# Gated linear attention loop: the score matrix of a token block computed in 64-token pieces, two of them side by side in the array

## The chip, the cores and the metric

The kernel runs on one core of one Trainium2 chip. The metric is device time in microseconds of one execution; lower is better. The time before is 1255.59 us, the median of three runs (1254.0 to 1257.15).

## The reference, cut to what matters

The program is one step of a two-layer backbone on 256 context tokens and 1024 latent tokens of width 1024. Layer 0 mixes tokens by gated linear attention (4 heads, key width 128, value width 256, both directions over the tokens), layer 1 by grouped-query softmax attention. The change is in layer 0. For a chunk of tokens the reference computes, with `b` the running sum of the log decays:

```python
qe = qi * jnp.exp(b)
ke = ki * jnp.exp(-b)
a = jnp.where(mask, jnp.einsum("bhtk,bhsk->bhts", qe, ke), 0.0)
o = jnp.einsum("bhts,bhsv->bhtv", a, vi) + jnp.einsum("bhtk,bhkv->bhtv", qe, S)
```

`a` is the score of each query token t against each key token s, kept where s is not after t (in the other direction: not before t). The kernel works on blocks of 128 tokens, so of the 128 x 128 scores of a block and direction one half is masked away, and one 64 x 64 quarter of it lies wholly in the masked half.

## The kernel before

The stages follow each other: modulation vectors and the first normalisation (to about 76 us), the loop `gla` of layer 0 (to about 518 us), the output projection of layer 0 with the first keys and queries of layer 1 (`gla_out`), the attention of layer 1 (`attention`), its output projection. The change touches the loop alone; the order of the instructions differs up to the first tiles of `gla_out` and is the same, instruction for instruction, from there on.

`gla` runs over head slots h = 0 to 4 and, in each, over the 10 token blocks of 128 (two of the context, eight latent). One step does, for head h: `intra` (the scores `a` and the transposed decayed keys of the block), `outer` and `local` (state update and first direction's output), and ahead of time `decay`, `decayed` and `value_gate` of later blocks; for head h - 1 it does `combine` (the other direction's scan, with its output matmul at L826) and `gated`. In h = 4 only `combine` of head 3 and the gates are left. Between these go projections for the next head (`qk_piece`), and a `filler`: matrix-vector products for the modulation (`gemv`, L391: eight f32 matmuls with weights of 32 columns, each in one of four column tiles of the array, by `tile_position=(0, 32 * j)`), weight splits, and the first output tiles. In the loop 40 blocks (4 heads x 10) call `intra`.

`intra` takes one PSUM bank of tag `kt` (one buffer): its first half receives the two transposed `ke` (L742), its second half, `ap`, the scores of both directions (L745). `ks` copies the first half out (L748), `copy_predicated` takes the unmasked scores (L753), GpSimd adds the directions (L754).

The names in the profile: `en` is `ke`, `kt` the bank, `wada` the gemv's weights, `Sc` the other direction's state, `oghl` and `hT_hi` parts of the output projection's input. L214 is the helper that issues the three f16 products of every split projection.

An f32 matmul shows in the trace as two passes, each with its own weight load; an f16 one as a single pass. PE is TensorE's matmuls, PEld its weight loads.

The order of the instructions on each engine is set by a scheduler that works on priorities (`TC = {"schedule_with_timeline_sim": True}`): code inside `with self.later("A"):` has its priority moved by `LATER["A"]`. So a changed number there, or a changed operation, moves instructions all through the loop.

Of the kernel before, what the change touches and what calls it, by code (L numbers as in the profile page):

```python
# [17 lines left out]
P = 128  # L18
# [5 lines left out]
NTP = TP // P  # L24
# [23 lines left out]
SECOND = 1  # L48

LATER = {  # L50
    "loc": -30,
    "kt": 30,
    "A": -15,
    "intra": -5,
    "ks": -90,
    "combine": -15,
    "cs": -20,
    "vg": -10,
    "u": 75,
    "gated": 50,  # L60
    "decay": -25,
    "outer": 10,
    "Uc": -100,
    "a9.qr": 30,
    "a.s1": 30,
    "gate": -5,
# [4 lines left out]
    "x.q": -15,  # L71
    "a0.qr": 40,
    "x.prep": -90,
    "oa": 30,
    "jobs": -20,
    "a.q": -210,
    "x.mod": 60,
# [6 lines left out]
    "a9.s1": -160,  # L84
    "a0.s1": 400,
    "pieces8": 95,
    "filler": -30,
    "a0.s0": 75,
    "at": -100,
    "a0.rest": 30,  # L90
# [23 lines left out]
    "eprep": 400,  # L114
    "z.out": -5,
    "x.kset": -30,
}

ADA = tuple((0, b) for b in (8, 9, 10, 11)) + tuple((1, b) for b in (4, 5, 6, 7, 0, 1, 2, 3, 8, 9, 10, 11))
# [8 lines left out]
class K:  # L128
# [603 lines left out]
    def intra(self, i, st):  # L732
        nc = self.nc
        ke, qe = st["ke"], st["qe"]
        kt, ap = (
            t.rearrange("p (d k) -> p d k", d=2)
            for b in (self.bank("kt"),)
            for t in (b[:, 0 : 2 * P], b[:, 2 * P :])
        )
        with self.later("kt"):  # L740
            for d in range(2):
                nc.tensor.transpose(kt[:, d, :], ke[:, d, :], self.ident)  # L742
        with self.later("A"):
            for d in range(2):
                nc.tensor.matmul(ap[:, d, :], ke[:, d, :], qe[:, d, :], start=True, stop=True)  # L745
        ks = self.t(self.ew, [P, 2, P], F32, "ks")
        with self.later("ks"):
            nc.vector.tensor_copy(ks, kt)  # L748
        am = self.am[self.ia % len(self.am)]
        self.ia += 1  # L750
        at = self.t(self.tl, [P, P], F32, "at", bufs=2)
        with self.later("at"):
            nc.vector.copy_predicated(am, self.mask, ap)  # L753
            nc.gpsimd.tensor_tensor(at, am[:, 0, :], am[:, 1, :], ALU.add)  # L754
        st["at"], st["ks"] = at, ks
# [108 lines left out]
    def gla(self, wq, w, filler):  # L864
# [6 lines left out]
        def ahead_decay(slot):  # L871
            h, n = divmod(slot, NT)
            if h < GH:
                g[slot] = self.decay(h, orders[h][n])
# [7 lines left out]
        def ahead_gate(slot):  # L882
# [7 lines left out]
                    self.inv_g[h - 1] = self.mulcol(self.inv_h, ws[h][2][1], self.gcp, f"inv_g{h % 2}")  # L890
            x[slot] = self.value_gate(h, orders[h][n], ws[h])

        for n in range(3):
            ahead_decay(n)
        ahead_decayed(0)
# [606 lines left out]
def emit(ctx, tc, I, O, dbg=None, stop=None):  # L1502
    k = K(ctx, tc, I, O, dbg)
    nc = tc.nc
# [27 lines left out]
    with ExitStack() as c:  # L1532
# [9 lines left out]
        with ExitStack() as c1:  # L1542
# [10 lines left out]
            def group(gi):  # L1553
                xs = []
                for j in range(GROUPS[gi][1]):
                    x = k.t(k.p1, [P, D], F32, "x", bufs=4)
                    load(x, xrow(I, GROUPS[gi][0] + j))
                    xs.append(x)
                return xs

            xs = group(0)
# [3 lines left out]
            for t in (*k.wtile(1)[0:2], *k.wtile(2)[0:2], k.hT_hi, k.hT_hi, k.hT_lo, k.hT_lo):  # L1565
                a = 4096 * (len(to) % 2) if len(to) > 3 else 0
                t = t.rearrange("p k n -> p (k n)")[:, a : a + 4096].bitcast(F32)
                n = len(to)
# [64 lines left out]
        wo, gm, prep, held, xs = [], [], [], [], []  # L1633


        def prompt(slot):
            h = [late[1][:, 512 * j : 512 * j + 512] for j in range(4)]
            if slot == 0:
                for kk in range(KT):
                    k.modulate(k.transpose(zs, kk, ("o", "U")[kk % 2]), kk, GROUPS[2][0], h=h[kk % 4])  # L1640
            elif slot < 3:
                k.qk_piece(0, slot - 1, 2, wq)
            else:
                k.rank_sum(*k.rank(2, h[0]))

        def filler(slot):
            if slot < 4:
                prompt(slot)
            if slot == 0:
                k.jobs.append(late_qk)  # L1650
            if slot == 2:
                k.fold_qk(1, wq)
            if slot in (9, 34):
                gm.append(k.mod_load(*((0, 2, 1) if slot == 9 else (1, 0, 3))))
            if slot in (10, 35):
                k.jobs.append(((k.gate_rows if slot == 10 else k.mod_rows_out), *gm.pop()))
            if slot % 2 == 0:
                if held:
                    k.gemv(*held.pop())
            elif queue:  # L1660
                held.append(k.ada_load(*queue.pop(0), k.t(k.ada, [P, KT, 256], F32, "wada")))
            if cols and slot in AHEAD:
                with tc.issue_after(first):
                    name, j, ap = cols.pop(0)
                    k.jobs.append((k.split_ahead, name, j, k.stage(ap)))
            if slot in WO:
                b = WO.index(slot)
                if b == 0:
                    k.w0 = k.wtile(0)
                if b < 2:  # L1670
                    t = [t[:, :, 256 * b : 256 * b + 256] for t in k.w0[0:2]]
                elif b == 2:
                    t = [t[:, :, 0:256] for t in k.nw[0:2]]
                else:
                    t = k.t(k.ada, [P, KT, 256], F32, "wada").rearrange("p k n -> p (k n)").bitcast(F16)
                    t = t.rearrange("p (j k n) -> p j k n", j=2, k=KT)
                    t = [t[:, 0], t[:, 1]]
                wo.append([*t, None])
                st = k.stage(I["gla_w_out"][b])
                k.jobs.append((k.placed, f"wo{b}", k.fill_out, wo[-1], st))  # L1680
            if slot == 40:
                k.gt = k.gate_load(0)
                k.iw = k.t(k.const, [P, 4], F32, "iw")
                for b, t in enumerate(wo):
                    nc.vector.tensor_copy(k.iw[:, b : b + 1], t[2])
                wo[:] = [(*k.w0[0:2], 512)] + [(hi, lo, 256) for hi, lo, _ in wo[2:]]
                t, k.gb = k.wtile(2)[0:2]
                t = t.rearrange("p k n -> p (k n)").bitcast(F32)
                for n in range(2):
                    xs.append(t[:, D * n : D * n + D])  # L1690
                    load(xs[n], xrow(I, NTP + n))
                k.rows_load(1)
            if slot in PREP:
                n = PREP.index(slot)
                a = k.t(k.wst, [P, KT, 256], F32, "wst").rearrange("p k n -> p (k n)")[:, 0:D]
                b = [k.t(k.qkp, [P, 512], F32, f"{j}{n % 2}").bitcast(F16) for j in "qk"]
                to = k.out_load(NTP + n, a, b)
                k.jobs.append((lambda *a: prep.append(k.placed("eprep", k.out_prep, *a)), *to))
            if slot in EARLY:
                n = EARLY.index(slot)  # L1700
                hT, lT, inv = prep[n]
                with k.later("eres"):
                    k.residual(
                        NTP + n, lambda j: (hT[:, j, :], lT[:, j, :]), wo, inv, xs[n], [k.bank("A"), k.bank("kt")]
                    )
                t = k.t(k.spl, [P, 2, KT // 2, 256], F16, "split").rearrange("p j k n -> p j (k n)")
                k.jobs.append((k.placed, "emod", k.early_mod, NTP + n, xs[n], (t[:, 0], t[:, 1])))

        k.gla(wq, wv, filler)
    if "og" in k.dbg:  # L1710
        load(k.dbg["og"], k.og_d)
# [3 lines left out]
    with ExitStack() as ca:  # L1715
# [15 lines left out]
        wo = []  # L1731
# [16 lines left out]
def xrow(I, i):  # L1748
    if i < NTP:
        return I["x_prompt"][0, i * P : i * P + P, :]  # L1750
    return I["x_sample"][0, (i - NTP) * P : (i - NTP) * P + P, :]
# [97 lines left out]
```

## Time and profile before

| | before |
|---|---|
| median of 3 runs | 1255.59 us (1254.0 to 1257.15) |
| profiled execution | 1256.39 us, its span 1254.6 us |
| mean granted TensorE clock | 0.993 |
| PE busy in the span | 1193.2 us (95%) |
| DVE, ACT, POOL busy | 942.8, 689.5, 326.6 us |
| the loop between 100 and 490 us | PE busy 388.46 of 390 us |
| L745 (scores), passes of PE | 160, mean 276 ns |

PE time in the profile is the union of modelled matmul spans, which overlap: a pass of 276 ns can follow the one before it after 110 ns. What a pass costs is therefore read from the distance between starts, not from its duration.

### The profile page before, as it was taken

To read this page: it belongs to the slowest core of one execution; us is meant where nothing else is said; L and a number is where in the kernel's file an instruction comes from. 1 tells how busy PE (TensorE), PEld (TensorE's weight loads), DVE (VectorE), ACT (ScalarE), POOL (GpSimd) and SP (SyncE) were. 2 spreads that over 40 slices of the span, in tenths; PEclk is the share of its full clock that TensorE was granted. 3 is DMA by queue.
4 is the path that set the end of the run, shared out by engine and by line. 5 is a ranking of instruction groups with operands and counts; after the bars stand their busy time and mean duration, and the time that the engine had idled before them with its cause. 6 is when DMAs were issued, how large, how long until landed. Compare 5 with 4: busy or idle time off the path is not lost. (4 is left out here: it accounts for less than half of the span.)

```text
span 1254.6 us, 22383 instructions
## 1 busy us (share of the span) xinstructions
PE 1193.2 (95%) x7990; PEld 781.4 (62%) x7990; DVE 942.8 (75%) x2188; ACT 689.5 (55%) x1698; POOL 326.6 (26%) x566
## 2 busy tenths in 40 slices
PE   4899999999999999898999899999999999989998
PEld 3467765655556557665776666767766657665444
DVE  4787879879788799769875687877766687785653
ACT  2664666647656567623333577666676676663110
POOL 0132123223321243311213434332232342310000
PEclk9999999999999999899999999999999999999999
DMA  9511565456555545589974887767868466978432
GB/s 377 194 65 73 202 210 191 160 176 207 164 180 179 159 124 164 142 237 248 260 191 130 182 157 132 140 132 151 185 135 151 110 123 132 195 139 208 163 135 84
DMA packets 317664, 209.74 MB, mean 167 GB/s; under 512 B 257094, under 2 KB 294254, under 8 KB 309232
## 3 DMA queue, kind: packets, MB, share of 16 engines
q1 hardware_dynamic: 310400, 190.78, 59.1%
q10 hardware_dynamic: 4688, 10.57, 2.4%
q0 software_dynamic: 2464, 6.95, 1.9%
q8 instruction: 63, 1.03, 0.3%
q14 instruction: 49, 0.40, 0.1%
HBM read 107.57 MB, written 39.35 MB: 117 GB/s over the span
## 5 line engine op out<-in xcount | busy, mean ns | idle before, releaser
L214 PEld LDWEIGHTS <-hT_hi 128*128 128x128 f16 x1920 | 187.8, 98 | 120.6 <-DMA hT_hi<-oghl 3.8
L214 PE MATMUL mm<-whi,hT_hi 128*128 128x512 f16 (+1 forms) x576 | 200.2, 348 | 0.5 <-ACT gx L679 0.4
L214 PE MATMUL mm<-whi,hT_lo 128*128 128x512 f16 (+1 forms) x576 | 200.3, 348 | 0.0
L214 PE MATMUL mm<-wlo,hT_hi 128*128 128x512 f16 (+1 forms) x560 | 194.2, 347 | 0.9 <-DVE wlo L276 0.9
L214 PEld LDWEIGHTS <-whi 128*128 128x128 f16 x1232 | 120.2, 98 | 63.8 <-issue 4.4
L1285 PE MATMUL S<-kT,wst 128*128 128x512 f16 (+1 forms) x624 | 140.2, 338 | 7.1 <-ACT p L1293 6.1
L214 PE MATMUL mm<-hT_hi,whi 128*128 128x256 f16 (+1 forms) x480 | 141.0, 294 | 3.7 <-ACT gx L1328 2.4
L1318 DVE SCALAR_TENSOR_TENSOR phl<-p,srec,phl 128x1280 f16<-128x1280 f32 (+1 forms) x80 | 107.0, 1337 | 49.5 <-ACT phl L1317 33.3
L214 PE MATMUL mm<-hT_lo,whi 128*128 128x256 f16 (+1 forms) x480 | 141.0, 294 | 0.0
L214 PE MATMUL mm<-hT_hi,wlo 128*128 128x256 f16 (+1 forms) x480 | 141.0, 294 | 0.0
L214 PEld LDWEIGHTS <-hT_lo 128*128 128x128 f16 x960 | 94.2, 98 | 62.5 <-issue 1.3
L214 PE MATMUL mm<-PT,vh 128*128 128x256 f16 x672 | 117.9, 279 | 9.3 <-DMA PT<-phl 6.3
L1288 DVE TENSOR_REDUCE smx<-S 128x1 f32<-128x1280 f32 (+1 forms) x80 | 101.3, 1271 | 27.0 <-PE S L1285 26.9
L1293 ACT ACTIVATE p<-S,snb,sexp 128x1280 f32<-128x1280 f32 (+1 forms) x80 | 99.1, 1238 | 12.6 <-DVE phl L1318 7.2
L1285 PEld LDWEIGHTS <-wst 128*128 128x128 f16 x624 | 60.9, 98 | 57.3 <-issue 7.1
L214 PE MATMUL mm<-PT,vl 128*128 128x256 f16 x336 | 93.9, 279 | 0.0
L1315 POOL TENSOR_SCALAR phl<-p,srec 128x1280 f16<-128x1280 f32 (+1 forms) x40 | 52.8, 1319 | 107.0 <-DVE srec L1309 62.7
L214 PEld LDWEIGHTS <-vh 128*128 128x128 f16 x672 | 66.7, 100 | 21.1 <-issue 6.0
L214 PEld LDWEIGHTS <-wlo 128*128 128x128 f16 x616 | 60.2, 98 | 29.8
L1124 POOL TENSOR_TENSOR rope<-hx,ropet 128x64 f32<-128x64 f32 x160 | 53.3, 363 | 84.0 <-ACT hx L1249 61.6
L237 DVE TENSOR_REDUCE wmx<-wst 128x1 f32<-128x512 f32 x104 | 65.1, 675 | 3.0 <-DMA wst<-in_att_w 2.0
L205 POOL TENSOR_TENSOR hrs<-hrsa,mhalf 128x2 f32<-128x2 f32 x50 | 39.5, 792 | 81.2 <-DVE hrsa L203 80.7
(383 smaller groups left out, 2682.7 us busy)
## 6 DMA issues: line engine op xcount, KB each, us to landing
wada<-in_w_ada SPq DMA_DIRECT2D x16, 1024.0 KB, 5.4
wst<-in_att_w SPq DMA_DIRECT2D x14, 1024.0 KB, 5.4
wst<-in_gla_w_in SPq DMA_DIRECT2D x12, 1024.0 KB, 5.3
og_d<-gx SPq DMA_DIRECT2D x40, 128.0 KB, 1.9
og_d<-og POOLq DMA_DIRECT2D x40, 128.0 KB, 3.0
wst<-og_d SPq DMA_DIRECT2D x5, 1024.0 KB, 6.1
xr<-x_d SPq DMA_DIRECT2D x9, 512.0 KB, 3.8
out<-xr ACTq DMA_DIRECT2D x17, 256.0 KB, 2.0
```

Of the source, the lines that this page charges most:

```text
L205: nc.gpsimd.tensor_tensor(r, a, self.mhalf[:, 0:w], ALU.pow)
L214: self.pe = self.nc.tensor.matmul(out, a, b, start=k == 0 and j == 0, stop=k == n - 1 and j == 2).ins
L237: nc.vector.tensor_reduce(mx[:, j : j + 1], st[:, 2 * j : 2 * j + 2, :], AX.XY, ALU.max, apply_absolute_value=True)
L1124: nc.gpsimd.tensor_tensor(tv[:, h, :, w, :], xv[:, h, :, 1 - w, :], sn[:, :, w, :], ALU.mult)
L1285: nc.tensor.matmul(S[:, a : a + n], x, y, start=m == 0, stop=m == 2)
L1288: last = nc.vector.tensor_reduce(mx, S, AX.X, ALU.max).ins
L1293: nc.scalar.activation(p, S, AF.Exp, scale=self.sexp, bias=nb, accum_out=den)
L1315: nc.gpsimd.tensor_scalar(hi, p, r, 2.0 ** 14, ALU.mult, ALU.mult)
L1318: nc.vector.scalar_tensor_tensor(lo, p, r2, hi, ALU.mult, ALU.subtract)
```

## The change

The full product of 128 keys by 128 queries becomes, for each direction, a matmul of all 128 keys by the 64 queries that need both halves of the keys, and one of 64 keys by the other 64 queries, which sits in one half of the array's columns (`tile_position=(0, 64 * d)`); the halves of the two directions are different ones. The quarter that the mask removes is set to zero once ahead of the loop. For that the bank `kt` is taken once and kept (`self.kt`). Eleven numbers of `LATER` change or are new.

```diff
 LATER = {
-    "loc": -30,
+    "loc": -5,
-    "A": -15,
-    "intra": -5,
+    "A": -30,
+    "intra": -150,
...
+    "decayed": 5,
+    "z": -100,
 }
...
         kt, ap = (
             t.rearrange("p (d k) -> p d k", d=2)
-            for b in (self.bank("kt"),)
+            for b in (self.kt,)
             for t in (b[:, 0 : 2 * P], b[:, 2 * P :])
         )
...
         with self.later("A"):
+            h = P // 2
             for d in range(2):
-                nc.tensor.matmul(ap[:, d, :], ke[:, d, :], qe[:, d, :], start=True, stop=True)
+                b = slice(h - h * d, P - h * d)
+                nc.tensor.matmul(ap[:, d, b], ke[:, d, :], qe[:, d, b], start=True, stop=True, skip_group_check=True)
+            for d in range(2):
+                b = slice(h * d, h * d + h)
+                nc.tensor.matmul(
+                    ap[b, d, b], ke[:, d, b], qe[:, d, b], start=True, stop=True,
+                    tile_position=(0, h * d), skip_group_check=True,
+                )
...
+        self.kt = self.bank("kt")
+        ap, h = self.kt[:, 2 * P :], P // 2
+        self.nc.vector.memset(ap[h:P, 0:h], 0.0)
+        self.nc.vector.memset(ap[0:h, P + h :], 0.0)
         for n in range(3):
             ahead_decay(n)
```

Three places show what moves in the order of PE's instructions. Line numbers of the changed kernel are two higher up to L745, and ten higher from L754 on: L744 is the transpose, L749 the matmul of 64 queries by all keys, L752 the quarter, L393 the gemv, L836 the output matmul of `combine`, L216 the projections.

A block in the middle of the loop (head 2, fifth of its ten), before: PE's transposes (`kt<-ident`) and scores (`kt<-qe,en`) among a projection into `mm`.

```order
L214 LDWEIGHTS hT_hi_73
L214 MATMUL mm_4362<-whi_711_2930,hT_hi_73 128x512
L742 MATMUL kt_4325<-ident_81,en_4205 128x128
L214 LDWEIGHTS hT_hi_73
L214 MATMUL mm_4362<-wlo_712_2931,hT_hi_73 128x512
L742 MATMUL kt_4325<-ident_81,en_4205 128x128
L745 MATMUL kt_4325<-qe_4210,en_4205 128x128 x2
L214 LDWEIGHTS hT_lo_74
L214 MATMUL mm_4362<-whi_711_2930,hT_lo_74 128x512
```

The same block in the changed kernel.

```order
L216 LDWEIGHTS hT_hi_73
L216 MATMUL mm_4254<-whi_697_2948,hT_hi_73 128x512
L744 MATMUL kt_794<-ident_81,en_4232 128x128 x2
L749 MATMUL kt_794<-qe_4237,en_4232 128x64 x2
L752 MATMUL kt_794<-qe_4237,en_4232 64x64 x2
L216 LDWEIGHTS hT_hi_73
L216 MATMUL mm_4254<-wlo_698_2949,hT_hi_73 128x512
L216 LDWEIGHTS hT_lo_74
L216 MATMUL mm_4254<-whi_697_2948,hT_lo_74 128x512
```

The two score matmuls have become four, and the quarters stand between instructions that use the whole array. After the 40 pairs of quarters an f16 weight load follows 25 times, a gemv 5 times, and an f32 or bf16 weight load 10 times.

A gemv, before, in PE's order in head 1, between a projection and the next block's decay sums (`cs`).

```order
L214 LDWEIGHTS hT_lo_74
L214 MATMUL mm_2555<-whi_328_1521,hT_lo_74 128x512
L391 MATMUL mm_2637<-wada_2497,cst_166 32x256 x8
L719 LDWEIGHTS ghi_2406
L719 MATMUL cs_2672<-cum_142,ghi_2406 128x130
L719 LDWEIGHTS glo_2407
L719 MATMUL cs_2672<-cum_142,glo_2407 128x130
```

The same gemv in the changed kernel.

```order
L393 MATMUL mm_2653<-wada_2512,cst_166 32x256 x3
L744 MATMUL kt_794<-ident_81,en_2549 128x128 x2
L696 LDWEIGHTS r_140
L696 MATMUL z_2558<-wa_28_141,r_140 128x256
L393 MATMUL mm_2653<-wada_2512,cst_166 32x256 x3
L749 MATMUL kt_794<-qe_2554,en_2549 128x64 x2
L752 MATMUL kt_794<-qe_2554,en_2549 64x64 x2
L393 MATMUL mm_2653<-wada_2512,cst_166 32x256 x2
```

The gemv's eight matmuls now stand in three pieces, with full-width matmuls and a pair of quarters between them. Over the loop the 16 gemvs stand in 17 pieces before and in 24 now.

The end of the loop (head slot 4), before: PE's output matmuls of `combine` (from `Sc` into the banks o, U, z, cs in turn), between projections for the gates.

```order
L214 LDWEIGHTS hT_lo_74
L214 MATMUL mm_6748<-whi_1555_5986,hT_lo_74 128x256
L826 MATMUL o_6680<-Sc_6676,qe_6278 128x256
L826 MATMUL U_6731<-Sc_6727,qe_6141 128x256
L826 MATMUL z_6786<-Sc_6782,qe_6010 128x256
L826 MATMUL cs_6855<-Sc_6851,qe_5893 128x256
L826 MATMUL o_6920<-Sc_6916,qe_5759 128x256
L214 LDWEIGHTS hT_hi_73
L214 MATMUL mm_6817<-whi_1555_5986,hT_hi_73 128x256
```

The same place in the changed kernel, up to the first matmul that has come between; 24 such matmuls of a gate projection (128x256) stand there.

```order
L216 LDWEIGHTS hT_lo_74
L216 MATMUL mm_6736<-whi_1521_6024,hT_lo_74 128x256
L836 MATMUL o_6723<-Sc_6719,qe_6319 128x256
L836 MATMUL U_6774<-Sc_6770,qe_6181 128x256
L216 LDWEIGHTS hT_hi_73
L216 MATMUL mm_6791<-whi_1521_6024,hT_hi_73 128x256
```

Behind the last of the 24 it goes on like this.

```order
L216 LDWEIGHTS hT_lo_74
L216 MATMUL mm_6791<-whi_1521_6024,hT_lo_74 128x256
L836 MATMUL z_6829<-Sc_6825,qe_6049 128x256
L836 MATMUL cs_6898<-Sc_6894,qe_5931 128x256
L836 MATMUL o_6963<-Sc_6959,qe_5796 128x256
L216 LDWEIGHTS hT_hi_73
L216 MATMUL mm_6860<-whi_1521_6024,hT_hi_73 128x256
```

One gate projection has moved from behind the five output matmuls to between the second and the third. The gate projections of the last blocks all end earlier than before, and on SyncE's queue the last store of a gated block (`og_d<-gx`) now stands ahead of the reloads for the output projection (`og<-og_d`), where one stood behind them.

More of the change, by code (lines that the diff above doesn't have):

```diff
@@ L57 @@
     "cs": -20,
-    "vg": -10,
+    "vg": 15,
     "u": 75,
@@ L62 @@
     "outer": 10,
-    "Uc": -100,
+    "Uc": -125,
     "a9.qr": 30,
@@ L73 @@
     "x.prep": -90,
-    "oa": 30,
+    "oa": 25,
     "jobs": -20,
@@ L86 @@
     "pieces8": 95,
-    "filler": -30,
+    "filler": -55,
     "a0.s0": 75,
@@ L1703, in filler @@
                     k.residual(
-                        NTP + n, lambda j: (hT[:, j, :], lT[:, j, :]), wo, inv, xs[n], [k.bank("A"), k.bank("kt")]
+                        NTP + n, lambda j: (hT[:, j, :], lT[:, j, :]), wo, inv, xs[n], [k.bank("A"), k.kt]
                     )
```

## The prediction

> **What bounds the kernel now.** I read the page's busy times first, then the busy times of the loop's stretch, then the groups of the lines that change, and last the timeline of PE and PEld around them.
>
> ```profile
> span 1254.6 us, 22383 instructions
> PE 1193.2 (95%) x7990; PEld 781.4 (62%) x7990; DVE 942.8 (75%) x2188; ACT 689.5 (55%) x1698; POOL 326.6 (26%) x566
> 100.00:490.00 390.00, 388.46 (x2394) 239.38 (x2393) 324.15 (x882) 243.89 (x639) 113.45 (x200) 1.00 0.52 172
> L745 PE MATMUL kt<-qe,en 128*128 128x128 f32 x160 | 25.5, 276 | 0.0
> ```
>
> The third row is the loop from 100 to 490 us: PE is busy for 388.46 of 390 us at a granted clock of 1.00; DVE, the next, for 324.15. The fourth says that PE never stood idle ahead of a score matmul. So in the loop time is what PE's instructions take, and another order can give back 1.5 us there at most. The question is whether the four new matmuls cost PE less than the two old ones.
>
> **The change part by part.** Old price of a block. First PE, then PEld, the weight loads beside it:
>
> ```profile
> 300.94 0.59 PE L812 MATMUL A<-Sa,qe 128*128 128x256 f32 x2
> 301.37 0.59 PE L826 MATMUL o<-Sc,qe 128*128 128x256 f32 x2
> 302.02 0.61 PE L745 MATMUL kt<-qe,en 128*128 128x128 f32 x4
> 302.47 0.27 PE L694 MATMUL z<-wa,r 98*128 98x256 f16 x1
> 302.58 0.38 PE L214 MATMUL mm<-whi,hT_hi 128*128 128x512 f16 x1
> ```
>
> ```profile
> 301.92 0.53 PEld L745 LDWEIGHTS kt<-qe,en 128*128 128x128 f32 x4
> 302.36 0.10 PEld L694 LDWEIGHTS <-r 98*128 98x128 f16 x1
> ```
>
> The four passes of L745 hold PE from 302.02 to 302.47: 0.45 us, 0.11 each, and 40 x 0.45 = 18 us in all. Two f32 passes of 256 columns take 301.37 - 300.94 = 0.43, so an f32 pass streams 128 columns in 0.108 us and 64 in 0.054. The four loads follow each other at 0.11 too (0.44 from the first to the next group's). So with 128 columns load and pass are equally long, and with 64 the load is the longer. That a load is not hidden where the array has no earlier work of the kind to hide it shows behind a gemv:
>
> ```profile
> 284.46 0.27 PE L694 MATMUL z<-wa,r 98*128 98x256 f16 x1
> 284.66 1.07 PE L391 MATMUL mm<-wada,cst 128*32 128x256 f32 x16
> 285.66 0.70 PE L770 MATMUL U<-v,ks 128*128 128x256 f32 x2
> 496.32 0.60 PE L770 MATMUL U<-v,ks 128*128 128x256 f32 x2
> L391 PE MATMUL mm<-wada,cst 128*32 128x256 f32 x256 | 17.3, 385 | 0.0
> ```
>
> The two passes of L770 take 0.70 there and 0.60 among ordinary work: 0.10 us is the bare load of 128 f32 columns.
>
> *All keys by 64 queries.* Two matmuls, four passes, each with a fresh load of 128 columns. The first load hides under the pass ahead of it; then three steps at the pace of the loads and one bare stream: 3 x 0.11 + 0.054 = 0.385 us. Half the columns have saved only 0.065.
>
> *Into and out of the divided array.* The f16 pass at 284.46 has 256 columns, worth 0.11 (302.47 to 302.58), so the gemv could start at 284.57 and starts at 284.66: 0.09 us lost. Its 16 passes take 1.07 with a last pass of 0.38, so the last starts at 285.35; it streams 0.215 and could hand over at 285.565, but L770 starts at 285.66: 0.095 lost. Then the next load is bare: 0.10 for f32 or bf16 weights (10 of the 40 places), little for f16. The trace has this only for tiles of 32 columns; I take the same for 64. The Trainium skill, "TensorEngine Tiling (Array Packing)", Key Properties, says that a change of tiling mode of any kind drains the engine; the trace agrees with its 0.09 and 0.095, and no run here shows 64 columns yet.
>
> *The quarters.* One after the other the gemv's 16 passes would take 16 x 0.215 = 3.4 us; they take about 0.9, so column tiles do run side by side. Two tiles of two passes: a bare load of 64 columns, half of 0.10, then 2 x 0.054: 0.16 us; 0.11 more if the two tiles do not overlap.
>
> Sum for a block: 0.385 + 0.09 + 0.16 + 0.095 + 0.03 (10 x 0.10 over 40 blocks, rounded up for the f16 loads) = 0.76, against 0.45: +0.31 us, and 40 x 0.31 = +12.4 us on PE.
>
> *Gemvs cut in pieces.* Seven more pieces than before. Each costs another 0.19 of changes and, as its eight matmuls no longer fill four column tiles, about one more round of 0.215: 7 x 0.4 = +2.8 us. Together +15.2 us on the engine that bounds the loop; nothing covers it, since PE is what the others wait for.
>
> *The end of the loop.* Here PE waits in series for the scan of `combine`, which goes through GpSimd and DVE:
>
> ```profile
> 501.17 0.60 PE L826 MATMUL o<-Sc,qe 128*128 128x256 f32 x2
> 503.13 0.70 PE L826 MATMUL U<-Sc,qe 128*128 128x256 f32 x2 [1.36 <-POOL Sc L791]
> 504.68 0.70 PE L826 MATMUL z<-Sc,qe 128*128 128x256 f32 x2 [0.85 <-POOL Sc L791]
> 507.03 1.22 PE L826 MATMUL cs<-Sc,qe 128*128 128x256 f32 x2 [1.65 <-POOL Sc L791]
> 508.88 1.22 PE L826 MATMUL o<-Sc,qe 128*128 128x256 f32 x2 [0.63 <-POOL Sc L791]
> 509.89 0.42 PE L214 MATMUL mm<-whi,hT_hi 128*128 128x256 f16 x1
> 510.10 0.42 PE L214 MATMUL mm<-wlo,hT_hi 128*128 128x256 f16 x1
> 513.09 0.31 PE L214 MATMUL mm<-whi,hT_hi 128*128 128x256 f16 x1
> ```
>
> The chain from the first to the fifth output matmul lasts 7.7 us and stays. In it the changed order puts a gate projection, 24 passes at 0.11 = 2.6 us, that ran behind it: -2.6 us. Behind these waits the 15 f16 passes up to 513.09 are 0.21 apart instead of 0.11 (the clock has dropped): with shorter waits that 1.6 us may go as well. I take -3.5 us, between 0 (the scan slips too) and -5. The wait that is late next is the third of the chain, for the fifth matmul.
>
> *Behind the loop.* PE waits twice more:
>
> ```profile
> 570.96 0.23 PE L172 MATMUL kv<-ident,amx 128*128 128x128 bf16 x1 [1.81 <-DVE p2e L183]
> 579.67 0.39 PE L214 MATMUL y<-whi,hT_hi 128*128 128x512 f16 x1 [3.50 <-DMA hT_hi<-oghl]
> 558.44 4.45 SPq L839 DMA_DIRECT2D og_d<-gx  x1
> ```
>
> In the changed order 37 key projection passes that filled PE between these two (0.11 each, 4.0 us) come after the second. Against that, SyncE's queue no longer holds the store of the third row, which blocked it for 4.45 us ahead of the transposes that the second wait is for. I take 0, between -3.5 and +4.0.
>
> *The rest.* Two `memset` on DVE, once: at most two of its 0.42 us copies of 128 x 256, while PE has projections to do: 0, at most 0.8. The kept bank: there was one buffer before as well, so the next block's transposes wait for the same reads; 0, and no gain either, as PE never waited for it (0.0 in its row). The smaller query columns change nothing for DVE, which still reads all of `ap`.
>
> Sum: 1256.4 (the profiled execution) + 15.2 - 3.5 = 1268.1 us. That execution was 0.8 above the median of the three runs, so **1267.3 us** is forecast. A measurement of this kernel can tell about 0.3%, 3.8 us, from no change.
>
> **The rivals.**
>
> *The pieces cost only their columns* (ends faster). If loads keep pace and the array takes the quarters without a stop, a block needs 4 x 0.054 + 2 x 0.054 = 0.32 us instead of 0.45: -5.0 us; with the cut gemvs' rounds (7 x 0.215 = 1.5) and the loop's end, -7.0: 1248.6 us. It decides from where bare loads and both changes of mode together fall below 0.12 us a block. For it speaks that the gemv's tiles overlap so well; against it that every gemv in the trace is met by the two gaps, and the 0.70 of L770. Chance 0.15.
>
> *Passes start before their load is done.* Then the 64-query passes go at 0.054, not 0.11: 40 x 3 x 0.056 = 6.7 us less, 1260.6 us. The Trainium skill, "TensorE: Matmul & The Clock Gate", Architectural detail, says that a matmul can begin on sub-arrays that are loaded while others are still loading. The 0.70 of L770 speaks against it here, since a whole load is seen there. Chance 0.10.
>
> *The quarters run one after the other*, and the waits at the end of the loop stay: +0.11 x 40 = 4.4 and no 3.5: 1275.2 us; the pair would not do what it is placed for. The gemv speaks against it, though its tiles are narrower. Chance 0.12.
>
> **How the numbers follow.** The forecast has 0.63: 1267.3 with -1.5 to +4 for its unknown ends. The range of 1256 to 1276 takes in the slower rivals and the lower edge of the second, and leaves out the first (0.15) and little else. Faster by over 0.3% (below 1251.8): 0.15. Within 0.3%: 0.07, mostly the second rival with all of the 5 us at the loop's end. Slower: 0.78.
>
> **What would show it.** Right: starts of the 128x64 passes 0.11 apart; about 0.09 free ahead of each pair of 64x64 and as much behind; the stretch from 100 us to the last `intra` some 14 us longer, PE as full as before; the waits for `Sc` near 503 to 509 us reduced to two or three. Wrong: 128x64 passes 0.055 apart, quarters starting where the last pass's stream ends, or the loop as long as before; or new waits of PE inside the loop, which would make it dearer than any case here.

## The result and the profile after

The changed kernel takes 1272.07 us (median of 4 runs, 1270.03 to 1274.42) against 1254.80 (1253.83 to 1257.15) for the kernel before, measured on the same chip: 1.0135 times the time, with a 95% interval of 1.011 to 1.0161. That is 17.3 us slower. The forecast was 1267.3 us, 11.7 us above the median that it started from, in a range of 1256 to 1276. The profiled execution of the changed kernel took 1274.42 us, 18.0 more than the one of before.

The page's first lines, the stretch of the loop, and the groups of the two lines that compute the scores (L749 all keys by 64 queries, L752 the quarters), with the first and last start of each:

```profile
span 1272.6 us, 22698 instructions
PE 1209.8 (95%) x8150; PEld 788.8 (62%) x8150; DVE 941.8 (74%) x2190; ACT 687.8 (54%) x1698; POOL 324.4 (25%) x566
100.00:490.00 390.00, 388.89 (x2438) 235.03 (x2437) 311.71 (x846) 233.98 (x609) 107.82 (x191) 1.00 0.51 166
L749 PE MATMUL kt<-qe,en x160: 217/275/323, 89.9 to 504.9; 128*128 128x64 f32 x160
L752 PE MATMUL kt<-qe,en x160: 222/246/271, 90.4 to 505.2; 128*64 128x64 f32 x160
```

PE is as full as before (388.89 of 390 us), and DVE, ACT and GpSimd have less to do in the same stretch: the loop has slowed down, bound by PE. For before the same group read:

```profile
L745 PE MATMUL kt<-qe,en x160: 272/275/377, 91.2 to 493.6; 128*128 128x128 f32 x160
```

From the first score pass to the last it was 402.5 us; it is 415.3, 12.8 more. One block in the timeline of PE, with the f16 passes around it, and PE's weight loads beside it:

```profile
265.96 0.38 PE L216 MATMUL mm<-whi,hT_hi 128*128 128x512 f16 x1
266.17 0.56 PE L749 MATMUL kt<-qe,en 128*128 128x64 f32 x4
266.66 0.34 PE L752 MATMUL kt<-qe,en 128*64 128x64 f32 x4
266.92 0.39 PE L216 MATMUL mm<-wlo,hT_hi 128*128 128x512 f16 x1
```

```profile
265.96 0.63 PEld L749 LDWEIGHTS kt<-qe,en 128*128 128x128 f32 x4
266.65 0.20 PEld L752 LDWEIGHTS kt<-qe,en 128*64 128x64 f32 x4
```

From 266.17 to 266.92 the block holds PE for 0.75 us; before it was 0.45. Step by step, from one pass's start to the next, that is 0.058, 0.112, 0.112, then 0.205 to the first quarter, 0.107 to the second round of quarters, and 0.161 from there to the next work. The loads of the quarters begin at 266.65 and not, as those of the first matmuls do, under the passes ahead of them.

The rest of the loss lies behind the loop. PE's waits from the end of the loop to the first output tiles, the passes around the longest one, and the granted clock there (the last columns of a stretch's row are the clock, the DMA share and the GB/s):

```profile
PE kv L174 <- DVE amx L1194: 7.3, 1, 7.3
PE y L216 <- DMA hT_hi<-oghl: 4.2, 1, 4.2
PE y L216 <- DVE whi L996: 1.8, 1, 1.8
```

```profile
581.77 0.27 PE L216 MATMUL y<-wada,hT_lo 128*128 128x256 f16 x1
589.32 0.29 PE L174 MATMUL kv<-ident,amx 128*128 128x128 bf16 x1 [7.28 <-DVE amx L1194]
589.40 0.42 PE L216 MATMUL kv<-whi,hT_hi 128*128 128x256 f16 x1
589.62 0.42 PE L216 MATMUL kv<-wlo,hT_hi 128*128 128x256 f16 x1
...
590.68 0.42 PE L216 MATMUL kv<-whi,hT_hi 128*128 128x256 f16 x1
595.35 0.61 PE L216 MATMUL y<-whi,hT_hi 128*128 128x512 f16 x1 [4.25 <-DMA hT_hi<-oghl]
```

```profile
590.00:600.00 10.00, 5.75 (x22) 2.67 (x20) 6.42 (x11) 1.38 (x3) 0.00 (x0) 0.52 1.09 234
```

The prediction had two of these waits at 1.81 and 3.50 us. Now they are 7.28 and 4.25, and after them PE's passes of 256 columns stand 0.21 us apart instead of 0.11, at a granted clock of 0.52. From the last pass of the early residuals (548.04 before, 558.55 after) to the first score pass of the attention, the stretch is 152.9 us long before and 163.5 after:

```profile
L1285 PE MATMUL S<-kT,wst x624: 269/379/379, 700.9 to 1126.5; 128*128 128x512 f16 x96, 128*128 128x256 f16 x60
L1299 PE MATMUL S<-kT,wst x624: 269/379/379, 722.1 to 1144.7; 128*128 128x512 f16 x96, 128*128 128x256 f16 x60
```

So the 18.0 us of the two profiled executions are: -1.4 ahead of the loop (first transpose at 89.36 instead of 90.73), +11.9 in the loop and its end, up to the last early residual, +10.6 behind it, and -3.1 in the attention and what follows.

### The profile page after: what moved, and what is told of

Read it like the earlier page. It is cut to its first block, busy times and chain, and to the rows that moved or that the text cites. A ratio compares the mean times of both kernels' runs of the same rounds, so it can differ in the third digit from the quotient of the medians.

```text
span 1272.6 us, 22698 instructions
## 1 busy us (share of the span) xinstructions
PE 1209.8 (95%) x8150; PEld 788.8 (62%) x8150; DVE 941.8 (74%) x2190; ACT 687.8 (54%) x1698; POOL 324.4 (25%) x566
## 4 chain that ended last, share of the span: by engine, by line
PE 69%; DMA 10%; DVE 9%; ACT 5%; issue 2%; SPq 1%; POOL 1%; ACTq 0%; POOLq 0%; DVEq 0%
PE mm L216 37%; PE y L216 12%; PE S L1299 6%; DMA PT<-phl 5%; PE kv L216 3%; PE A L822 2%; PE mm L393 1%; SPq L490 1%; PE kt L749 1%; DMA wst<-og_d 1%; PE U L780 1%; PE U L776 1%; DVE smx L1302 1%; DMA wst<-xhl 1%; PE o L836 1%
## 5 line engine op out<-in xcount | busy, mean ns | idle before, releaser
L216 PEld LDWEIGHTS <-hT_hi 128*128 128x128 f16 x1920 | 187.1, 98 | 125.6 <-issue 7.6
L216 PE MATMUL mm<-whi,hT_hi 128*128 128x512 f16 (+1 forms) x576 | 199.5, 347 | 0.7 <-ACT gx L681 0.7
L216 PE MATMUL mm<-whi,hT_lo 128*128 128x512 f16 (+1 forms) x576 | 199.6, 347 | 0.0
L216 PE MATMUL mm<-wlo,hT_hi 128*128 128x512 f16 (+1 forms) x560 | 193.5, 346 | 0.9 <-DVE wlo L278 0.9
L216 PEld LDWEIGHTS <-whi 128*128 128x128 f16 x1232 | 120.3, 98 | 64.6 <-issue 4.4
L216 PE MATMUL mm<-hT_hi,whi 128*128 128x256 f16 (+1 forms) x480 | 141.0, 294 | 3.9 <-ACT gx L1342 3.3
L216 PE MATMUL mm<-hT_lo,whi 128*128 128x256 f16 (+1 forms) x480 | 141.0, 294 | 0.0
L216 PE MATMUL mm<-hT_hi,wlo 128*128 128x256 f16 (+1 forms) x480 | 141.0, 294 | 0.0
L216 PEld LDWEIGHTS <-hT_lo 128*128 128x128 f16 x960 | 94.1, 98 | 64.5 <-issue 3.9
L216 PE MATMUL mm<-PT,vh 128*128 128x256 f16 x672 | 116.3, 277 | 8.5 <-DMA PT<-phl 5.6
L216 PE MATMUL mm<-PT,vl 128*128 128x256 f16 x336 | 93.1, 277 | 0.0
L216 PEld LDWEIGHTS <-wlo 128*128 128x128 f16 x616 | 60.2, 98 | 29.7
L216 PEld LDWEIGHTS <-vh 128*128 128x128 f16 x672 | 66.2, 99 | 19.4 <-DMA PT<-phl 5.7
```

The costliest lines, as they stand in the source:

```text
L216: self.pe = self.nc.tensor.matmul(out, a, b, start=k == 0 and j == 0, stop=k == n - 1 and j == 2).ins
```

## The experiments: what a block costs

The table gives, for every kernel that was run, the time over that of before on the same chip, then three figures of its profiled execution: the length of the loop from first to last score pass, the median time from the first score pass of a block to the next pass of other work, where the block was not cut in two, and the stretch behind the loop against before's 152.9 us.

| kernel | ratio (95%) | loop, us | block, us | behind the loop, us |
|---|---|---|---|---|
| before | 1 | 402.5 | 0.447 | 0 |
| changed | 1.0135 (1.011 to 1.0161) | +12.8 | 0.754 | +10.6 |
| pieces, old numbers | 1.013 (1.0097 to 1.0162) | +17.4 | 0.754 | +3.8 |
| new numbers, whole matmuls | 1.0065 (1.0043 to 1.0088) | +3.2 | 0.446 | +4.6 |
| two halves over all keys | 1.0162 (1.0124 to 1.0201) | +18.3 | 0.840 | +3.5 |
| whole, and a pair of quarters | 1.0089 (1.0058 to 1.012) | +16.8 | 0.807 | +4.9 |
| whole, and two pairs | 1.0221 (1.0192 to 1.025) | +31.2 | 0.924 | +3.2 |
| halves without quarters | 1.0075 (1.0056 to 1.0094) | +1.0 | 0.393 | +3.0 |
| changed, rows on SyncE | 1.0125 (1.0102 to 1.0149) | +12.1 | 0.754 | +8.1 |
| before, rows on SyncE | 1.0006 (0.9993 to 1.0018) | +1.4 | 0.447 | +6.0 |
| changed, one number back | 1.013 (1.0101 to 1.0159) | +12.0 | 0.754 | +5.4 |
| changed, `loc` back | 1.0128 (1.0095 to 1.0161) | +12.3 | 0.754 | +6.0 |
| changed, once more | 1.0174 (1.014 to 1.0209) | +12.0 | 0.754 | +13.6 |

The stretch between the first and the last score pass doesn't hold the same work in every kernel: beside scores and gemvs it has 2087 passes before and 2050 in the changed kernel, where 37 have moved behind it (4.0 us of their columns). Up to the last early residual all kernels have the same 2423, except the one with `loc` back, which has 2418. From the first score pass to that point before takes 456.9 us; the changed kernel takes 11.7 more, the pieces with old numbers 16.1, the new numbers with whole matmuls 3.4, the one pair 15.7, the two pairs 30.8, the halves alone 5.1.

**The pieces with the old numbers.** The diff's `LATER` table taken back, all else kept.

> The pieces of after with all eleven order numbers of before (the scheduler then places them by itself: 19 gemv pieces against 17 before and 24 after; on DVE the key scale amx is ready ahead of the residual that waits for a transfer, as in before). Price theory (a block costs PE 0.75 us instead of 0.45): from the first transpose of the loop to the last score 12 to 13 us longer than before, total 1266 to 1269 us. Order theory (the time went into the refitted order): total 1253 to 1258 us.

1271.68 us, 1.013 times. The block is the same 0.754, so its price belongs to the pieces and not to the order. But the loop is 17.4 us longer and not 12.8 (expected 12 to 13), and the time is 2.7 us above the expectation: the refitted numbers save 4.6 us in the loop, 4.4 over equal work. They cost 6.8 behind it, and the two kernels take the same time.

**The new numbers with whole matmuls.** Before's score matmuls, the changed `LATER` table.

> The order numbers of after with the whole 128x128 score matmuls of before (23 gemv pieces; amx early on DVE). Price theory: the loop within 3 us of before (six more gemv pieces at 0.4), no long wait of PE for amx behind it, total 1253 to 1259 us. Order theory: 1268 to 1273 us.

1264.31 us, 1.0065 times: between the two expectations. The pieces carry more of the change's cost than the order does, but the order has a price of its own on blocks that it was not fitted to: the block stays at 0.446, the loop grows by 3.2 us and the stretch behind it by 4.6. The gemvs stand in 23 pieces instead of 17 and, counted from the first pass of a piece to the next other work, take 19.9 us instead of 16.2; the loop's other changes nearly cancel.

**Two halves over all keys.** In the kernel before, each matmul of 128 queries in two of 64, all in the whole array:

```
-                nc.tensor.matmul(ap[:, d, :], ke[:, d, :], qe[:, d, :], start=True, stop=True)
+                for b in (slice(0, h), slice(h, P)):
+                    nc.tensor.matmul(ap[:, d, b], ke[:, d, :], qe[:, d, b], start=True, stop=True, ...)
```

> Before, with each 128-query score matmul cut in two of 64 queries over all keys, in the whole array: eight passes a block instead of four, no divided array at all. If the weight load sets the pace (0.11 us a pass however few columns stream): 40 x 4 x 0.11 = +17 us in the loop, total 1270 to 1274 us. If a pass costs its columns (0.054): loop unchanged, 1253 to 1258 us.

The same columns in twice the passes, from PE's timeline, with the weight loads in the first row:

```profile
313.10 0.97 PEld L747 LDWEIGHTS kt<-qe,en 128*128 128x128 f32 x8
313.20 1.00 PE L747 MATMUL kt<-qe,en 128*128 128x64 f32 x8
314.04 0.27 PE L694 MATMUL z<-wa,r 98*128 98x256 f16 x1
```

Eight passes in 0.84 us: the second starts 0.058 behind the first, whose load was hidden, and every other 0.112 behind the one before it, though a pass streams 0.054. Their loads start 0.11 apart as well: the load sets the pace. A fixed price of any pass isn't it: f16 passes of 130 columns, each with its own load, follow each other at 0.06 us in the loop of before (L719). The loop is 18.3 us longer (expected 17), and the kernel takes 1275.23 us, 1.2 above the expectation.

**Halves without quarters.** Only the first half of the edit: a block has the two matmuls of 64 queries over all keys, and zeros where the quarters stood.

> The kernel before with only the 64 queries of each half that need all keys (in the whole array, no tiles, order numbers of before); the quarters, that is, half of the scores within the 64-token pieces, are left out, and zeros stand in their place. Load theory (a 64-column f32 pass takes 0.11 us, as long as its weights take to load, not the 0.055 of its columns): a block takes 0.385 instead of 0.45, loop -2.6 us against before, time within 4 us of before. Column theory (half the columns, half the time): a block takes 0.23, loop -9 us.

```profile
244.80 0.56 PE L747 MATMUL kt<-qe,en 128*128 128x64 f32 x4
245.19 0.38 PE L214 MATMUL mm<-whi,hT_lo 128*128 128x512 f16 x1
```

0.39 us, against 0.45 with twice the columns; columns alone would make it 0.23. Half of every score matrix left out saves 0.05 us a block, 2.2 in the loop. The loop did not get shorter even by that: it is 1.0 us longer than before, with nine more passes of other work in it, and the kernel takes 1266.12 us, which is outside the expected 4 us of before. Up to the last early residual PE's idle time is 9.6 us instead of 7.6, and slow passes behind those waits cost some 3.4 more than before. The block is thus as the load theory has it, and the time is not.

**Whole matmuls with a pair of quarters, and with two.** The matmuls of before, and behind them the quarters once or twice, which write what stands there already.

> Before, with the two quarters of after computed once more behind the whole score matmuls (same values, same place): the price of the divided array alone. Price theory: 0.09 + 0.16 + 0.095 + 0.03 = 0.375 us a block, +15 us in the loop, total 1268 to 1272 us. If the divided array cost only its columns (0.11 us): +4.4 us, 1258 to 1261 us.

> The kernel before with the redundant pair of quarters issued twice behind each whole matmul (one more pair than in the run with one). Change theory (each block pays 0.095 us into the 64-column mode and 0.095 out of it, once, and 0.107 for each round of two tiles): two more rounds, 40 x 2 x 0.107 = 8.6 us more than with one pair, first transpose to last score +25 against before. Rival, quarters one after the other: four more single passes of 0.107, +17 more, +34. Rival, the cost is the change alone: the same as with one pair, +17.

1266.59 and 1284.42 us. The blocks of the one and of the other:

```profile
311.37 0.61 PE L745 MATMUL kt<-qe,en 128*128 128x128 f32 x4
311.91 0.34 PE L749 MATMUL kt<-qe,en 128*64 128x64 f32 x4
312.18 0.28 PE L694 MATMUL z<-wa,r 98*128 98x256 f16 x1
```

```profile
359.79 0.61 PE L745 MATMUL kt<-qe,en 128*128 128x128 f32 x4
360.33 0.45 PE L749 MATMUL kt<-qe,en 128*64 128x64 f32 x8
360.72 0.39 PE L214 MATMUL mm<-wlo,hT_hi 128*128 128x512 f16 x1
```

0.81 and 0.93 us: the first pair costs 0.36 over before's block, the second 0.12 (medians of 0.807 and 0.924). Change theory is right that the mode is paid for once, and wrong about the price of a round. In the trace the passes of the two tiles start 6 to 8 ns apart, the second round 0.106 us behind the first, and the third and fourth 0.06 behind those. Only the first round of a pair shows a load; after it, two tiles side by side go at the pace of their columns. So of the pair's 0.36 us about 0.12 are work, and 0.24 are getting in and out, the first load among it. With one pair the loop is 16.8 us longer (expected 15), but the time is 1.4 us below the expected 1268; in its profile the stretch from the attention to the end took 9.2 us less than in before. With two it is 31.2 longer, nearer to the 34 of quarters one after the other than to the 25 of change theory; but quarters one after the other would have made the block 0.43 dearer and not 0.12. Of the further 14.4 us, 4.7 are those of 40 such blocks. The longer blocks were cut apart oftener by other passes, and PE changed its mode 180 times up to the last early residual instead of 139: all runs of score passes together take 8.2 us more. Gemvs, waits and slower passes make up the rest, and no run here separates them.

## The experiments: what lies behind the loop

The order on GpSimd is part of the answer. The two rows that load sample tiles (`xr`) stand behind the `nt_r` of the second early tile in the changed kernel, and ahead of it before. First before, then changed:

```profile
543.81 0.55 POOL L205 TENSOR_TENSOR nt_r<-nt_ra,mhalf 128x1 f32<-128x1 f32 x1 [17.60 <-DVE nt_ra L203]
544.31 1.34 POOL L1024 DMA_DIRECT2D xr<-in_x_sample  x2
559.68 0.56 POOL L205 TENSOR_TENSOR nt_r<-nt_ra,mhalf 128x1 f32<-128x1 f32 x1 [14.02 <-DVE nt_ra L203]
```

```profile
557.60 0.55 POOL L207 TENSOR_TENSOR nt_r<-nt_ra,mhalf 128x1 f32<-128x1 f32 x1 [22.77 <-DVE nt_ra L205]
571.81 0.55 POOL L207 TENSOR_TENSOR nt_r<-nt_ra,mhalf 128x1 f32<-128x1 f32 x1 [13.66 <-DVE nt_ra L205]
572.32 1.34 POOL L1038 DMA_DIRECT2D xr<-in_x_sample  x2
```

The loads go out 28 us later, of which 14 are the end of the loop and the early tile that came later, and 14 the wait of the second `nt_r` on the same queue. On DVE the output tile's residual then waits for them, and the key maxima (`amx`), for which PE waits 7.28 us, come behind that:

```profile
580.61 0.69 DVE L996 TENSOR_TENSOR xr<-y,xr 128x512 f32<-128x512 f32 x1 [2.65 <-DMA xr<-in_x_sample]
589.11 0.16 DVE L1194 TENSOR_SCALAR amx<-amx 128x2 f32<-128x2 f32 x1
```

**The sample rows on SyncE's queue**, in the changed kernel and, as a control, in the one before.

```
-                (nc.gpsimd if n < n0 + 2 else nc.sync).dma_start(xs[n], xrow(self.I, order[n]))
+                nc.sync.dma_start(xs[n], xrow(self.I, order[n]))
```

> The changed kernel, whose first two sample tiles of the stage behind the loop are loaded through SyncE's queue instead of GpSimd's, where they stand behind the second early tile's nt_r and are issued at 572.32 us (before: 544.31). Queue theory (the 10.7 us behind the loop come from the load that stands behind that nt_r: VectorE waits 2.65 us for it, the key maxima come late, TensorE waits 7.3 us for them): the load is issued near 569, VectorE's wait for xr and most of the 7.3 us go, last early residual to third output tile shrinks by 4 to 7 us, and the kernel takes 1265 to 1268. Rival, early-tile theory (ScalarE's wait of 7.75 us for the transposes of the first early tile sets it, the load is hidden): that stretch stays within 2 us and the kernel at 1270 to 1273. The loop itself is left as it is: first transpose to last score +13 against before in both.

> Control: the kernel before with the same two loads on SyncE's queue. There GpSimd issued them at 544.31, ahead of the second nt_r; SyncE has them behind the transposes of the first early tile, near 555. Both theories: no gain; the loop unchanged, the stretch behind the loop 0 to +4 us, so that a gain of the changed kernel from the same edit comes from where the load stood in its queue, not from the queue itself.

In the changed kernel the first load went out at 570.82, 1.5 us earlier and no more: on SyncE it stands behind a transpose (`hT_lo<-k`) that holds the queue from 568.34 to 570.78. DVE's wait for it is gone and the stretch behind the loop fell from +10.6 to +8.1, between the 2 us of the rival and the 4 of the queue theory; the time, 1271.42 us, lies in the rival's bounds. In the control the load goes out at 555.41 instead of 544.31, and the stretch behind the loop is 6.0 us longer in the profiled execution, but the ten timed runs do not differ from before's (1256.83 us, 1.0006). So this pair decides little.

**One number back.** `"decayed"` from 5 to 0 leaves the blocks and the 24 pieces of the gate rows, and puts the loads ahead of the second `nt_r`.

> The changed kernel with one number of its order table put back ("decayed" 5 to 0): the blocks and the 24 pieces of the gate rows stay, but on GpSimd the two loads of the sample rows stand ahead of the second early tile's nt_r again, and TensorE has 115 passes of the output product ahead of the key maxima instead of 144. Order theory (the 10.7 us behind the loop come from where the order puts the loads and the maxima): the loads are issued near 558 to 562 instead of 572, the stretch from the last early residual to the third output tile falls from +10.7 to about +4 as with the old numbers, first transpose to last score stays at +12 to +14, and the kernel takes 1264 to 1268. Rival, it follows from the later end of the loop and not from the order: +9 to +11 again, 1270 to 1273.

```profile
558.54 0.55 POOL L207 TENSOR_TENSOR nt_r<-nt_ra,mhalf 128x1 f32<-128x1 f32 x1 [21.01 <-DVE nt_ra L205]
559.04 1.34 POOL L1038 DMA_DIRECT2D xr<-in_x_sample  x2
PE kv L174 <- DVE p2e L185: 7.1, 1, 7.1
PE y L216 <- DVE whi L996: 1.9, 1, 1.9
```

The loads go out at 559.04, and the stretch is +5.4 us, near the +4 that was expected; the loop is where it was, +12.0. The time is 1270.74 us, 3 to 7 above the expectation, on a chip on which the unedited changed kernel (last in this section) took 1276.37. PE still waits 7.1 us once, now for another scale (`p2e`), but the second wait of 4.2, for `hT_hi<-oghl`, is gone; one of 1.0 for `hT_lo<-oghl` is left.

**Another number back.** `"loc"` from -5 to -30.

> The changed kernel with another number of the table put back ("loc" -5 to -30): the gate rows come in 22 pieces instead of 24, the two loads on GpSimd ahead of the second nt_r, and TensorE has 174 passes of the output product ahead of the key maxima. Order theory: behind the loop +3 to +6 instead of +10.7; loop +12 to +16, since the blocks are as in the changed kernel; 1264 to 1270. If the 0.75 us of a block are what the change costs, no order of these brings it below 1262.

The loads at 556.69, behind the loop +6.0 us, blocks of 0.754, 1271.05 us in all: as expected for the parts, and 1 us above the expected time. Here PE's long wait is one of 6.2 us for `hT_hi<-oghl`, so the order also chooses what PE waits for.

**The changed kernel once more.**

> The changed kernel once more, unedited, as the control of both on the same chip: 1270 to 1274, blocks of 0.754 us. If the stretch behind the loop differs from +10.7 by more than 3 us in this profiled execution, part of that figure belongs to the one execution and not to the order.

1276.37 us (1273.41 to 1279.33), on a chip on which before took 1254.91. Behind the loop it is +13.6, with the loads at 575.99 and these waits:

```profile
PE kv L174 <- DVE amx L1194: 7.2, 1, 7.2
PE y L216 <- DMA hT_hi<-oghl: 5.3, 1, 5.3
```

The blocks repeat to the nanosecond (0.754), the stretch behind the loop repeats in kind and not in size. Three kernels with the changed blocks and the loads ahead of the second `nt_r` lie at +3.8 to +6.0; two executions with the loads behind it at +10.6 and +13.6; with the loads on SyncE it is +8.1. The order, not the later end of the loop, makes this difference of some 5 to 10 us: the pieces with the old numbers end their loop 5 us later still, and lie at +3.8. Putting a number back also moves the maxima on DVE and the passes of PE ahead of them, so the share of the loads alone stays open.

The first 3 to 6 us are there in every other profile. PE executes the same 449 passes up to the third output tile in all but one of these kernels; what differs is waits and slow passes. In before it stands idle for 6.0 us there and no pass is slow. In the other kernels it stands idle for 5.9 to 16.7 us, and 1.4 to 3.9 us more go into passes at about half the clock behind the waits. Before was profiled once, so how far its 152.9 us repeat isn't shown; in the control, whose timed runs equal before's, the stretch was 6.0 us longer in the one execution profiled.

## Why the prediction was right, and where it was not

- **A block** (0.76 against 0.45): 0.754 against 0.447. The parts hold as well. Halves alone take 0.394, which is three steps of 0.112 and a stream of 0.058; the quarters start at 0.487, so 0.09 is free ahead of them; the two tiles run at once, a first round of 0.107 (a bare load of 0.05 and a stream) and a second whose columns take 0.054; and about 0.1 is lost behind. One term lies elsewhere: the 0.03 for the bare load of the next work isn't in the 0.754 but in the passes behind it, where an f32 pass of 256 columns lasts 0.105 longer, and an f16 or bf16 one 0.01 (I had put bf16 with f32). Together that is about 1.0 us over the loop.
- **The loop with its end** (+12.4, +2.8 and -3.5, together +11.7): +11.9, measured from the first transpose to the last early residual. That the two agree so closely is in part luck, since two terms were mis-sized and nearly cancel. The runs of score passes are 12.0 us longer in sum (30.4 against 18.4), with 1.0 behind them. The cut gemvs take 3.7 more (20.0 against 16.2; by the modelled spans below 21.6 against 17.3), so a further piece costs about 0.5 and not 0.4. The end of the loop gave back 5.4 and not 3.5: PE's idle time fell from 7.6 to 4.8 us, and the 18 slow passes that cost before 2.6 us between 500 and 515 are gone. The granted clock was 0.66 there and is 1.00 now, where before waits for the scan from 505 to 515 us and the changed kernel from 515 to 525. What is left for all else is 11.9 - 13.0 - 3.7 + 5.4 = 0.6.

The gemvs of the changed kernel, the end of the loop before, and in the changed kernel:

```profile
L393 PE MATMUL mm<-wada,cst 128*32 128x256 f32 x256 | 21.6, 386 | 0.0
505.00:515.00 10.00, 7.72 (x36) 5.06 (x35) 7.37 (x24) 5.34 (x20) 6.56 (x11) 0.66 0.31 95
515.00:525.00 10.00, 8.31 (x63) 6.87 (x64) 8.37 (x26) 6.82 (x25) 7.51 (x12) 1.00 0.45 139
```

- **Behind the loop** (0, between -3.5 and +4.0): this is the step that failed; it measured +10.6, far beyond its end of +4.0. I weighed PE's 37 projection passes and SyncE's store. I did not follow GpSimd's queue, where two loads had been moved behind an instruction that waits 13.66 us, nor the maxima on DVE behind them; and I did not ask what a longer wait does to the clock.
- **The rest** (0): -1.4 ahead of the loop and -3.1 behind it. The attention was not edited, and against before the stretch from its first score pass to the end changed by -9 to +2 us from kernel to kernel. The traces show most of what goes with it: from that pass on the granted clock was at half for three stretches of 3.41 us in before, two in the changed kernel, none with one pair (-9.2) and four with the halves alone (+2.1). Without PE's idle time the attention and what follows take 534.0, 532.1, 529.1 and 535.6 us in these four, so each such stretch costs about 1.6 us. PE's idle time itself, 15.4 to 20.3 us, makes the rest, and why it differs stays open.
- **The rivals.** That pieces cost only their columns is refuted by the block of 0.754; inside the mode, from the second round on, it is true. That 64-query passes go at 0.054 because they start before their load is done falls with the 0.84 us of eight half passes and with the 0.39 of four. For a pass that follows another at once, no run here shows a gain from the early start that the Trainium skill describes ("TensorE: Matmul & The Clock Gate", Architectural detail). The record of a half pass does begin 0.056 behind that of its load, but the steps stay at 0.112, the pace of the loads. Quarters one after the other: they start 6 to 8 ns apart.

The chance of 0.78 for slower stood on the loop, and the loop carried it. Against the profiled execution the sum of 1268.1 us fell 6.3 short: 10.6 missed behind the loop, less the 4.5 that the start and the attention gave and I did not expect, and 0.2 in the loop. That the time stayed inside the range is luck: with those 4.5 us added the median would stand at 1276.6, just outside it.

## What to carry to other kernels

Half the columns are not half the time: where a pass streams shorter than its weights load (here 0.054 against 0.112 us), cutting it saves next to nothing, and a pair of small tiles pays some 0.24 us to get into the divided array and out before it does 0.12 of work. Such pieces want many rounds behind one change. When a table of order numbers is refitted, read every queue behind the place it was fitted for, down to the two loads on the least busy engine; and give an order's side effects behind the loop a range of several us, since two executions of the same kernel differed there by 3.

## What the runs showed of the hardware that I had not expected

- Two f32 tiles of 64 columns side by side run at 0.06 us a round from the second pair on, their loads hidden, while f32 passes that stream the same 64 columns through the whole array stay at 0.112.
- The clock falls behind a wait, and the price of a wait is more than its length. Behind the 7.28 us it was 0.52 from 590 to 600 us, and passes stood 0.21 apart up to 599.5. The Trainium skill, "TensorE: Matmul & The Clock Gate", Part 1, puts the drop to half the rate after an idle window of about 3.4 us; the trace agrees for the 7.28, and for the 1.81 of before, behind which no pass is slow. But a wait of 3.50 in before cost no clock, and one of 2.58 with a pair of quarters did (0.58 from 590 to 600 us), so the length of a single wait doesn't decide it here (the columns behind the busy times are the granted clock, the DMA share and the GB/s):

```profile
580.00:590.00 10.00, 10.00 (x72) 6.77 (x70) 9.59 (x34) 5.01 (x12) 4.48 (x6) 1.00 0.97 295
590.00:600.00 10.00, 8.11 (x29) 3.45 (x27) 8.86 (x30) 3.69 (x7) 0.55 (x1) 0.58 1.08 275
```

The first row is before, behind its wait of 3.50 us at 579.67; the second is the kernel with one pair of quarters, behind its wait of 2.58 at 586.98. What decides it in these traces is where the wait falls. In each trace the granted clock changes only at times that lie whole multiples of 3.41 us apart, so an execution is divided into fixed stretches of 3.41 us; in before one begins at 513.15, where the clock comes back, and so others at 574.59 and 578.00. The wait of 3.50 is cut by the border at 578.00, and PE is busy for 1.58 and 1.74 us of the two stretches. The wait of 2.58 falls almost whole into one stretch, of which PE is busy for 1.28, and at the end of that stretch, 1.3 us behind the wait, the clock halves:

```profile
574.59:578.00 3.41, 1.58 (x15) 1.17 (x12) 1.48 (x2) 0.00 (x0) 0.00 (x0) 1.00 1.45 154
578.00:581.41 3.41, 1.74 (x11) 1.09 (x12) 3.41 (x8) 1.53 (x4) 0.00 (x0) 1.00 0.99 252
584.84:588.26 3.42, 1.28 (x13) 1.16 (x14) 3.38 (x17) 1.15 (x1) 0.56 (x1) 1.00 1.25 60
588.26:591.67 3.41, 2.63 (x15) 1.61 (x12) 1.08 (x3) 0.00 (x0) 0.00 (x0) 0.50 1.19 290
```

The first two rows are before, the last two the kernel with one pair. In the thirteen traces, between 60 and 1200 us, the clock halved behind every stretch at full clock in which PE stood idle for 2.02 us or more by the modelled spans, and behind none with less than 1.75; in between it did both. By this the same wait could cost clock in one execution and none in the next, which no run here tests by itself.
